# Keeping split weight pieces in DRAM between the two halves of the tokens

## The chip, the cores and the metric

The kernel runs on one core of a Trainium2 chip. The metric is the device time of one execution in microseconds. Engines are TensorE (PE, with its weight loads as PEld), VectorE (DVE), ScalarE (ACT), GpSimd (POOL) and SyncE (SP), which issues almost every DMA.

## The reference

One layer of a hybrid model with three branches on 2048 tokens of width 1024, in float32. Only the first lines matter for the change: the input projection to 8192 columns is the largest matrix product, and every branch reads pieces of it.

```python
h_lat = rmsnorm(x, norm_g) * (1.0 + sc_l) + sh_l
pl = split_proj(h_lat @ w_in + b_in)         # D_IN = 8192 columns
o_lat = neighbourhood_attention(q, k, v, k_c, v_c, rpb)   # 8 heads, 8 x 16 windows, 256 context keys
y_a = (a_b * short_conv(a_c * a_x, w_conv, b_conv) * silu(a_z)) @ w_br_a
y_f = (fourier_mix(f_u) * silu(f_z)) @ w_br_f
y_c = (attn_o * silu(c_z)) @ w_br_c
x_new = x + gt_l * ((sig(g_a) * y_a + sig(g_f) * y_f + sig(g_c) * y_c) @ w_out)
return rmsnorm(x_new, final_g)
```

## The kernel before

**Precision.** A float32 product is made of three matmuls of type fp32r. Each operand is split into a high part, which is a cast of it, and a low part, which is the operand less its high part. `split` (lines 130 to 132) does this: ScalarE casts (line 131), VectorE or GpSimd subtracts (line 132).

**The projection.** The 64 column blocks of w_in (128 columns each, 1024 deep, 512 KB) are taken two at a time. `pair(ma, mb, ...)` computes two blocks for 1024 tokens as a 2 by 2 block product with seven products in place of eight: the seven weight operands are a11, a12, a22 and four sums and differences of a11, a12, a21, a22, which GpSimd makes (lines 337 to 339 and 355). `piece` splits one of these into `wh` and `wl`, four buffers each; `P` runs its product, 12 matmuls over 512 tokens each (lines 310 to 312), into a PSUM bank; `evac` functions add the products together, apply bias and the nonlinearity, and store the result to DRAM. The token operands (B11, B21, B22, T1 to T4) are split once for each half of the tokens and stay in SBUF.

**The order of the work.** The tokens are done in two halves of 1024, and each half goes through the same 32 pairs: Q, K, V and the Fourier input, then the gated branches, then 12 gate pairs. In both halves every pair loads its two raw blocks from w_in (line 298, buffers `wr`, three of them) and makes and splits all seven pieces. Besides the pairs:

- start-up computes the modulation and normalises the first half, between the first two pairs (`first_pair`)
- in the first half, `small_work` makes gate vectors and the tables of the attention bias (`tbl`, line 736) between products
- near the end of the first half the token operands of the second half are made (`Prep`); the last pair of the half splits them in its hook
- in the second half, the 24 pairs after Q, K, V and Fourier run beside attention and then the Fourier transform, which are generators advanced by 2.7 steps for each product
- the last loop does the three branch products, the output product and the final norm for four blocks of 512 tokens

The framework places each engine's instructions in an order of its own, from a simulated time, and adds the waits; at run time each engine, and SP with its DMAs, goes through its list in order.

Of the kernel before, what the change touches and what calls it, by code (L numbers as in the profile page):

```python
# [11 lines left out]
F32 = mybir.dt.float32  # L12
F32R = mybir.dt.float32r
AF = mybir.ActivationFunctionType
ALU = mybir.AluOpType
# [44 lines left out]
def emit(tc, I, out, dbg=None):  # L60
    nc = tc.nc
# [4 lines left out]
    def pool(stack, name, bufs=1, space=None, side=None):  # L66
        kw = {} if space is None else {"space": space}
        if space is not DRAM:
            kw["reuse_waits"] = "tile"
        if side:  # L70
            return Aligned(stack, lambda n_, b_: tc.tile_pool(name=n_, bufs=b_, side=side, **kw), name, bufs)
        return stack.enter_context(tc.tile_pool(name=name, bufs=bufs, **kw))
# [4 lines left out]
    dr = pool(es, "dr", 1, DRAM)  # L77
# [4 lines left out]
    load = nc.sync.dma_start  # L82
    store = nc.sync.dma_start
    vtt = nc.vector.tensor_tensor
# [32 lines left out]
    state = {}  # L117
# [12 lines left out]
    def split(hi, lo, src, heng, leng):  # L130
        heng.copy(hi, src) if heng is nc.scalar else heng.tensor_copy(hi, src)  # L131
        return leng.tensor_tensor(lo, src, hi.bitcast(F32), ALU.subtract)  # L132
# [6 lines left out]
    wp = pool(ws_, "wp")  # L139
# [147 lines left out]

    def piece(src, leng, nm):  # L290
        wh = wp.tile([128, 512], F32R, tag="wh", name="wh" + nm, bufs=4)
        wl = wp.tile([128, 512], F32R, tag="wl", name="wl" + nm, bufs=4)
        split(wh, wl, src, nc.scalar, leng)
        return wh, wl

    def wraw_(m, p=None, bufs=3):
        t = (p or wp).tile([128, D], F32, tag="wr", name=f"wr{m}", bufs=bufs)
        load(t, I["w_in"][m])
        return t

    def wraw(m):
        t = wraw_(m)
        return t[:, :512], t[:, 512:]

    def prod(ps, w, name, first, last=True):
        op = state["op"]
        for k in KP:
            s = slice(k * 128, k * 128 + 128)
            oh, ol = op[name, k]
            nc.tensor.matmul(ps, w[0][:, s], oh, start=first and k == 0, stop=False)  # L310
            nc.tensor.matmul(ps, w[0][:, s], ol, start=False, stop=False)  # L311
            nc.tensor.matmul(ps, w[1][:, s], oh, start=False, stop=last and k == 3)  # L312

    def bank():
        return pm.tile([128, 512], F32, tag="mm", name="mm")

    def tmp():
        return wp.tile([128, 512], F32, tag="tp", name="tp", bufs=3)

    def P(w, name):  # L320
        p = bank()
        prod(p, w, name, True)
        return p

    def pair(ma, mb, evac, bg=None):
        bg = bg or (lambda: None)
        a11, a12 = wraw(ma)
        a21, a22 = wraw(mb)
        p = P(piece(a11, nc.vector, "1"), "B11")
        s1 = tmp()  # L330
        nc.scalar.copy(s1, p)
        bg()
        p = P(piece(a12, nc.vector, "2"), "B21")
        evac(0, 0, p, s1)
        bg()
        t1 = wp.tile([128, 512], F32, tag="ws", name="ws", bufs=1)
        ptt(t1, a21, a22, ALU.add)  # L337
        ptt(a21, a11, a21, ALU.subtract)
        ptt(a11, t1, a11, ALU.subtract)  # L339
        p = P(piece(a11, nc.vector, "6"), "T2")  # L340
        vtt(s1, p, s1, ALU.add)
        bg()
        p = P(piece(t1, nc.gpsimd, "5"), "T1")
        v = tmp()
        vtt(v, p, s1, ALU.add)  # L345
        bg()
        for _ in pair_end(evac, a11, a12, a21, a22, s1, v):
            bg()

    def pair_end(evac, a11, a12, a21, a22, u2, v):  # L350
        p = P(piece(a21, nc.gpsimd, "7"), "T3")
        evac(1, 1, p, v)
        vtt(u2, p, u2, ALU.add)  # L353
        yield
        ptt(a12, a12, a11, ALU.subtract)  # L355
        p = P(piece(a12, nc.gpsimd, "3"), "B22")
        evac(0, 1, p, v)
        yield
        p = P(piece(a22, nc.vector, "4"), "T4")
        evac(1, 0, p, u2)  # L360
        yield

    def first_pair(ma, mb, evac, raw, s1, t5):

        w = raw(ma)
        a11, a12 = w[:, :512], w[:, 512:]
        yield
        p = P(piece(a11, nc.vector, "1"), "B11")
        nc.scalar.copy(s1, p)
        yield  # L370
        w = raw(mb)
        a21, a22 = w[:, :512], w[:, 512:]
        yield
        t1 = wp.tile([128, 512], F32, tag="ws", name="ws", bufs=1)
        ptt(t1, a21, a22, ALU.add)
        ptt(a21, a11, a21, ALU.subtract)
        ptt(a11, t1, a11, ALU.subtract)
        p = P(piece(t1, nc.vector, "5"), "T1")
        vtt(t5, p, s1, ALU.add)
        yield  # L380
        p = P(piece(a12, nc.vector, "2"), "B21")
        evac(0, 0, p, s1)
        yield
        p = P(piece(a11, nc.vector, "6"), "T2")
        vtt(s1, p, s1, ALU.add)
        vtt(t5, p, t5, ALU.add)
        yield
        yield from pair_end(evac, a11, a12, a21, a22, s1, t5)


    def pre(dst, ps, add, m):
# [172 lines left out]
    def mod_end(k):  # L564
        row = rows.pop(k)
        pc_ = pe1.tile([128, 2, 2], F32, tag="pc", name="pc_")
        for s in range(2):
# [4 lines left out]
    state["op"], state["half"] = Operands(), 0  # L572
    raws = (lambda m: wraw_(m), lambda m: wraw_(m, ep, 2))
    gens = [first_pair(M_Q + 2 * n, M_Q + 2 * n + 1, ev_q((2 * n, 2 * n + 1)), raws[n],
                       tmp(), tmp() if n else scratch("T4", "l", 3, "t5"))
            for n in range(2)]
# [112 lines left out]
    for n_, p in enumerate(prs[2:]):  # L689
        (pair(*p))  # L690
        if n_ == 1:
            ex.close()
        if n_ >= 1:
            for m in (M_K, M_V):
                if n_ < 5:
                    ctx_tile(m + n_ - 1)
# [62 lines left out]
    for n_, p in enumerate(rest[:16]):  # L759
        (pair(*p, bg=lambda: bgs(0.5)))  # L760
# [31 lines left out]
    for p in rest[16:-1]:  # L792
        pair(*p, bg=lambda: bgn(RH))
# [390 lines left out]
    def load_wb(j, n_):  # L1184
        wr = c2.tile([128, 512], F32, tag="wr", name="wr", bufs=WRB)
        nc.sync.dma_start(wr, I["w_br"][j, n_])
        wh = c2.tile([128, 512], F32R, tag="wbh", name="wbh", bufs=3)
        wl = c2.tile([128, 512], F32R, tag="wbl", name="wbl", bufs=3)
        split(wh, wl, wr, nc.scalar, nc.gpsimd)
        return wh, wl  # L1190
# [31 lines left out]
    for b in range(NB):  # L1222
# [5 lines left out]
        for j in range(8):  # L1228
            acc = None
            for n_, br in enumerate("afc"):  # L1230
                wh, wl = wb0.pop(0) if wb0 else load_wb(j, n_)
# [134 lines left out]
```

## Time and profile before

| | |
|---|---|
| median of 3 runs | 2255.39 us (2252.5 to 2258.48) |
| profiled execution | 2256.13 us, span 2254.4 us |
| mean granted clock of TensorE | 0.985 |
| DMA | 336.78 MB, 149 GB/s on the mean |

The profile is taken from one execution. Busy time of an engine is the union of its instructions; a matmul of 512 columns is listed with about 0.39 us, but the next starts 0.23 us after it, so matmuls overlap in the list. A wait is put down to the instruction that released it. The granted clock is the share of full speed (2.4 GHz) that TensorE was given.

### The profile page before, as it was taken

What the parts mean: (1) busy time and instruction counts of PE and PEld (TensorE: products, weight loads), DVE (VectorE), ACT (ScalarE), POOL (GpSimd) and SP (SyncE); (2) the same over time, 40 slices, a digit from 0 to 9 for tenths busy, and PEclk for the clock granted to TensorE, in tenths of its full rate; (3) what the DMA queues carried; (4) which work ended last, traced back from release to release, by engine and by line L of the source; (5) the groups of instructions that cost most, each with busy time, mean ns of one, the idle gap of its engine ahead of it and who ended that gap; (6) DMA issues with size and microseconds to landing.
All of it is one profiled execution on the core that took longest, in us unless ns stands there. A gap on an engine that the chain in (4) does not pass through costs nothing. (4 is left out here: it accounts for less than half of the span.)

```text
span 2254.4 us, 32033 instructions
## 1 busy us (share of the span) xinstructions
PE 2132.9 (95%) x10588; PEld 1686.6 (75%) x10588; DVE 1547.0 (69%) x2731; ACT 887.1 (39%) x2011; POOL 1011.5 (45%) x761
## 2 busy tenths in 40 slices
PE   6899989999999899999999999999999898999998
PEld 4678768888788687777777777777757677878777
DVE  6864685565665665778787788786736868787773
ACT  3443222334544442454555555554213332222121
POOL 2753467654464654444444334343415243434341
PEclk8999999999999899999999999999999999999999
DMA  6244644233233344343444444453466676666561
GB/s 255 80 136 117 225 174 168 94 108 117 94 101 111 101 142 131 109 126 107 142 127 127 139 148 127 141 149 127 154 211 218 212 223 214 192 206 191 173 190 67
DMA packets 198863, 336.78 MB, mean 149 GB/s; under 512 B 22249, under 2 KB 89129, under 8 KB 197546
## 3 DMA queue, kind: packets, MB, share of 16 engines
q1 hardware_dynamic: 198554, 334.47, 46.8%
q8 instruction: 84, 1.38, 0.3%
q14 instruction: 81, 0.66, 0.1%
q10 hardware_dynamic: 144, 0.26, 0.0%
HBM read 248.27 MB, written 86.38 MB: 148 GB/s over the span
## 5 line engine op out<-in xcount | busy, mean ns | idle before, releaser
L131 ACT CAST wh<-wr 128x512 fp32r<-128x512 f32 x384 | 237.7, 620 | 479.1 <-PE mm L311 388.1
L132 DVE TENSOR_TENSOR wl<-wr,wh 128x512 fp32r<-128x512 f32 x256 | 244.7, 957 | 37.0 <-ACT wh L131 36.8
L132 POOL TENSOR_TENSOR wl<-wr,wh 128x512 fp32r<-128x512 f32 x128 | 173.7, 1360 | 212.8 <-ACT wh L131 191.0
L337 POOL TENSOR_TENSOR ws<-wr 128x512 f32<-128x512 f32 x62 | 89.0, 1435 | 309.0 <-DMA wr<-w_in 255.3
L395 DVE SCALAR_TENSOR_TENSOR st<-mm,bin,tp 128x512 f32<-128x512 f32 x158 | 118.0, 747 | 143.0 <-PE mm L312 136.0
L132 POOL TENSOR_TENSOR wbl<-wr,wbh 128x512 fp32r<-128x512 f32 x96 | 130.9, 1367 | 163.0 <-ACT wbh L131 160.4
L126 PE MATMUL mm<-yh,wbh 128*128 128x512 f32 x384 | 153.5, 400 | 17.8 <-DVE tg L1238 10.4
L128 PE MATMUL mm<-yh,wbl 128*128 128x512 f32 x384 | 152.8, 398 | 2.3 <-POOL wbl L132 2.3
L127 PE MATMUL mm<-yl,wbh 128*128 128x512 f32 x384 | 151.8, 396 | 0.3 <-DVE yl L132 0.3
L931 PE MATMUL tr<-ident,P 128*128 128x128 f32 (+3 forms) x672 | 120.4, 280 | 19.1 <-DVE PT L941 7.9
L132 POOL TENSOR_TENSOR wl<-ws,wh 128x512 fp32r<-128x512 f32 x62 | 83.7, 1350 | 112.5 <-ACT wh L131 94.8
L931 PEld LDWEIGHTS tr<-ident,P 128*128 128x128 f32 (+3 forms) x672 | 78.9, 139 | 68.4 <-DVE PT L941 25.4
L355 POOL TENSOR_TENSOR wr<-wr 128x512 f32<-128x512 f32 x64 | 87.9, 1373 | 93.7 <-DVE wl L132 58.8
L450 DVE TENSOR_TENSOR st<-mm,tp 128x512 f32<-128x512 f32 x96 | 65.9, 686 | 87.2 <-PE mm L312 84.4
L310 PE MATMUL mm<-B11h,wh 128*128 128x512 f32 x256 | 104.5, 408 | 14.0 <-DVE tp L353 7.4
L131 ACT CAST wbh<-wr 128x512 fp32r<-128x512 f32 x96 | 59.2, 620 | 127.6 <-PE mm L127 61.0
L126 PE MATMUL po<-wo,mh 128*128 128x512 f32 x256 | 101.2, 395 | 7.8 <-DVE xn L1261 7.7
L310 PE MATMUL mm<-T4h,wh 128*128 128x512 f32 x256 | 103.1, 403 | 4.5 <-DVE tp L345 4.5
L311 PE MATMUL mm<-B11l,wh 128*128 128x512 f32 x256 | 103.0, 402 | 4.2 <-DVE B11l L132 4.2
L339 POOL TENSOR_TENSOR wr<-ws,wr 128x512 f32<-128x512 f32 x62 | 84.3, 1360 | 49.6 <-DVE wl L132 36.3
L310 PE MATMUL mm<-B21h,wh 128*128 128x512 f32 x256 | 102.6, 401 | 3.6 <-DVE st L450 2.8
L310 PE MATMUL mm<-T2h,wh 128*128 128x512 f32 x256 | 102.8, 402 | 1.4 <-ACT T2h L131 1.4
(319 smaller groups left out, 6293.3 us busy)
## 6 DMA issues: line engine op xcount, KB each, us to landing
wr<-w_in SPq DMA_DIRECT2D x136, 512.0 KB
gd<-st SPq DMA_DIRECT2D x96, 256.0 KB
wr<-w_br SPq DMA_DIRECT2D x96, 256.0 KB
tg<-gd SPq DMA_DIRECT2D x96, 256.0 KB
tab<-dft SPq DMA_DIRECT2D x40, 256.0 KB
wa<-w_ada SPq DMA_DIRECT2D x32, 256.0 KB
rawq<-qd SPq DMA_DIRECT2D x64, 128.0 KB
rawk<-kd SPq DMA_DIRECT2D x64, 128.0 KB
```

Of the source, the lines that this page charges most:

```text
L126: nc.tensor.matmul(ps, ah, bh, start=first, stop=False)
L127: nc.tensor.matmul(ps, ah, bl, start=False, stop=False)
L128: nc.tensor.matmul(ps, al, bh, start=False, stop=last)
L131: heng.copy(hi, src) if heng is nc.scalar else heng.tensor_copy(hi, src)
L132: return leng.tensor_tensor(lo, src, hi.bitcast(F32), ALU.subtract)
L310: nc.tensor.matmul(ps, w[0][:, s], oh, start=first and k == 0, stop=False)
L311: nc.tensor.matmul(ps, w[0][:, s], ol, start=False, stop=False)
L337: ptt(t1, a21, a22, ALU.add)
L339: ptt(a11, t1, a11, ALU.subtract)
L355: ptt(a12, a12, a11, ALU.subtract)
L395: stt(dst, ps, bc(m), add, ALU.add, ALU.add)
L931: nc.tensor.transpose(pt[:w_, x * 128 : x * 128 + 128], src, ident)
```

## The change

In the first half `piece` splits into the two parts of one tile `w2` (four buffers) and stores that tile, 512 KB, into a DRAM tile of its own. In the second half `pair` makes no pieces: `pair_again` loads the kept piece for each of its seven products. Four of seven loads go to the buffers of `w2`, three to those of `wr`, which the raw blocks no longer need. The context keys and values (`ctx_tile`) still split their pieces, without a store. The products, their order and the evacuations are the same in the second half.

```diff
+    kept = {}
+
+    def piece(src, leng, nm, keep=None):
+
+        w = wp.tile([128, 2, 512], F32R, tag="w2", name="w2" + nm, bufs=4)
+        split(w[:, 0], w[:, 1], src, nc.scalar, leng)
+        if keep is not None:
+            kept[keep, nm] = d = dr.tile([128, 2, 512], F32, name=f"wd{keep}_{nm}")
+            store(d, w.bitcast(F32))
+        return w[:, 0], w[:, 1]
+
+    turn_ = iter(range(10 ** 6))
+
+    def again(ma, nm):
+        if next(turn_) % 7 < 4:
+            w = wp.tile([128, 2, 512], F32R, tag="w2", name="w2k", bufs=4)
+        else:
+            w = wp.tile([128, 2, 512], F32R, tag="wr", name="wrk", bufs=3)
+        load(w.bitcast(F32), kept[ma, nm])
+        return w[:, 0], w[:, 1]
...
     def pair(ma, mb, evac, bg=None):
         bg = bg or (lambda: None)
+        if state["half"]:
+            for _ in pair_again(ma, evac):
+                bg()
+            return
         a11, a12 = wraw(ma)
         a21, a22 = wraw(mb)
-        p = P(piece(a11, nc.vector, "1"), "B11")
+        p = P(piece(a11, nc.vector, "1", ma), "B11")
...
+    def pair_again(ma, evac):
+        p = P(again(ma, "1"), "B11")
+        s1 = tmp()
+        nc.scalar.copy(s1, p)
+        yield
+        p = P(again(ma, "2"), "B21")
+        evac(0, 0, p, s1)
+        yield
...
```

The other calls of `piece` in `pair`, `pair_end` and `first_pair` get the key `ma` in the same way, and `pair_again` goes on through the pieces 6, 5, 7, 3 and 4.

## Rows read from the trace of the kernel before

**Rows 1.** The page: span, then busy us, share of the span and instructions.

```profile
span 2254.4 us, 32033 instructions
...
PE 2132.9 (95%) x10588; PEld 1686.6 (75%) x10588; DVE 1547.0 (69%) x2731; ACT 887.1 (39%) x2011; POOL 1011.5 (45%) x761
```

**Rows 2.** Busy time by stage: stage, length, engines with instructions, granted clock, DMA share, GB/s.

```profile
0.00:115.00 115.00, 86.77 (x369) 68.82 (x369) 84.28 (x131) 49.45 (x85) 58.03 (x48) 0.93 0.48 168
...
240.00:353.00 113.00, 103.78 (x447) 81.39 (x447) 82.18 (x104) 29.10 (x51) 66.09 (x44) 0.98 0.62 213
353.00:582.00 229.00, 229.00 (x1012) 189.60 (x1012) 125.75 (x157) 82.45 (x133) 133.87 (x97) 1.00 0.33 110
582.00:758.00 176.00, 163.60 (x711) 133.65 (x710) 124.85 (x167) 87.73 (x145) 97.13 (x68) 0.95 0.30 98
758.00:918.00 160.00, 155.25 (x700) 127.59 (x699) 84.39 (x110) 56.65 (x103) 82.48 (x63) 1.00 0.43 132
918.00:1562.00 644.00, 622.42 (x3939) 476.28 (x3937) 515.08 (x1295) 346.15 (x1061) 266.90 (x204) 1.00 0.44 130
...
1704.00:1765.00 61.00, 59.62 (x269) 48.63 (x267) 44.30 (x74) 23.20 (x38) 28.41 (x21) 1.00 0.64 204
1765.00:1800.00 35.00, 26.77 (x101) 19.15 (x99) 27.48 (x41) 13.23 (x22) 8.38 (x6) 0.90 0.72 234
```

**Rows 3.** Waits of weight loads, 918 to 1562 us: total us, times, longest.

```profile
PEld po L953 <- issue: 35.1, 154, 0.4
PEld tr L931 <- DVE PT L941: 25.2, 65, 1.6
...
PEld tr L931 <- ACT PT L941: 6.4, 22, 0.5
PEld tr L931 <- DVE P L897: 6.3, 5, 2.8
```

**Rows 4.** Order of time in one gate pair of the first half.

```profile
563.68 1.30 POOL L132 TENSOR_TENSOR wl<-ws,wh 128x512 fp32r<-128x512 f32 x1 [1.75 <-ACT wh L131]
...
570.44 0.33 SPq L298 DMA_DIRECT2D wr<-w_in  x1
...
571.11 0.39 PE L310 MATMUL mm<-T1h,wh 128*128 128x512 f32 x1
...
573.83 0.39 PE L310 MATMUL mm<-T3h,wh 128*128 128x512 f32 x1
...
574.64 0.69 DVE L132 TENSOR_TENSOR wl<-wr,wh 128x512 fp32r<-128x512 f32 x1
574.64 1.82 POOL L337 TENSOR_TENSOR ws<-wr 128x512 f32<-128x512 f32 x1 [4.23 <-DMA wr<-w_in]
```

**Rows 5.** Groups of instructions, 758 to 1765 us: busy us, mean ns, idle before.

```profile
L131 ACT CAST wh<-wr 128x512 fp32r<-128x512 f32 x190 | 117.6, 620 | 215.5 <-PE mm L311 197.8 <-POOL wr L339 6.0 <-PE mm L312 4.3
L132 DVE TENSOR_TENSOR wl<-wr,wh 128x512 fp32r<-128x512 f32 x126 | 114.4, 908 | 13.7 <-ACT wh L131 13.6
...
L132 POOL TENSOR_TENSOR wl<-wr,wh 128x512 fp32r<-128x512 f32 x64 | 83.2, 1302 | 148.0 <-ACT wh L131 126.2 <-PE sl L886 5.6 <-DMA vt<-vd 5.3
L338 POOL TENSOR_TENSOR wr<-wr,wr 128x512 f32<-128x512 f32 x31 | 45.5, 1466 | 2.4
...
L132 POOL TENSOR_TENSOR wl<-ws,wh 128x512 fp32r<-128x512 f32 x32 | 41.9, 1308 | 86.9 <-ACT wh L131 69.9 <-PE sl L886 8.6 <-PE sx L883 4.8
L131 ACT CAST wh<-ws 128x512 fp32r<-128x512 f32 x32 | 19.8, 620 | 22.2 <-PE mm L311 22.2
```

**Rows 6.** The VectorE splits beside attention, 918 to 1562 us (four a pair).

```profile
L132 DVE TENSOR_TENSOR wl<-wr,wh 128x512 fp32r<-128x512 f32 x68 | 62.0, 912 | 0.0
```

**Rows 7.** Busy time in two shorter stretches, columns as in the stages above.

```profile
240.00:263.00 23.00, 23.00 (x114) 18.91 (x114) 13.32 (x17) 8.41 (x16) 14.36 (x11) 1.00 0.76 261
747.00:758.00 11.00, 7.21 (x16) 4.75 (x17) 9.28 (x12) 3.72 (x7) 6.33 (x5) 0.51 0.31 101
```

**Rows 8.** Waits of VectorE for the bias tables, 240 to 353 us.

```profile
DVE Bv L735 <- DMA tbl<-Bv: 9.7, 7, 2.3
```

More of the change, by code (lines that the diff above doesn't have):

```diff
@@ L332, in pair @@
         bg()
-        p = P(piece(a12, nc.vector, "2"), "B21")
+        p = P(piece(a12, nc.vector, "2", ma), "B21")
         evac(0, 0, p, s1)
@@ L339, in pair @@
         ptt(a11, t1, a11, ALU.subtract)
-        p = P(piece(a11, nc.vector, "6"), "T2")
+        p = P(piece(a11, nc.vector, "6", ma), "T2")
         vtt(s1, p, s1, ALU.add)
         bg()
-        p = P(piece(t1, nc.gpsimd, "5"), "T1")
+        p = P(piece(t1, nc.gpsimd, "5", ma), "T1")
         v = tmp()
@@ L346, in pair, with pair_end @@
         bg()
-        for _ in pair_end(evac, a11, a12, a21, a22, s1, v):
+        for _ in pair_end(ma, evac, a11, a12, a21, a22, s1, v):
             bg()
-    def pair_end(evac, a11, a12, a21, a22, u2, v):
-        p = P(piece(a21, nc.gpsimd, "7"), "T3")
+    def pair_end(ma, evac, a11, a12, a21, a22, u2, v):
+        p = P(piece(a21, nc.gpsimd, "7", ma), "T3")
         evac(1, 1, p, v)
@@ L355, in pair_end @@
         ptt(a12, a12, a11, ALU.subtract)
-        p = P(piece(a12, nc.gpsimd, "3"), "B22")
+        p = P(piece(a12, nc.gpsimd, "3", ma), "B22")
         evac(0, 1, p, v)
         yield
-        p = P(piece(a22, nc.vector, "4"), "T4")
+        p = P(piece(a22, nc.vector, "4", ma), "T4")
         evac(1, 0, p, u2)
+        yield
[6 more added lines that the diff above has]
+        evac(0, 0, p, s1)
+        yield
+        p = P(again(ma, "6"), "T2")
+        vtt(s1, p, s1, ALU.add)
+        yield
+        p = P(again(ma, "5"), "T1")
+        v = tmp()
+        vtt(v, p, s1, ALU.add)
+        yield
+        p = P(again(ma, "7"), "T3")
+        evac(1, 1, p, v)
+        vtt(s1, p, s1, ALU.add)
+        yield
+        p = P(again(ma, "3"), "B22")
+        evac(0, 1, p, v)
+        yield
+        p = P(again(ma, "4"), "T4")
+        evac(1, 0, p, s1)
         yield
@@ L367, in first_pair @@
         yield
-        p = P(piece(a11, nc.vector, "1"), "B11")
+        p = P(piece(a11, nc.vector, "1", ma), "B11")
         nc.scalar.copy(s1, p)
@@ L377, in first_pair @@
         ptt(a11, t1, a11, ALU.subtract)
-        p = P(piece(t1, nc.vector, "5"), "T1")
+        p = P(piece(t1, nc.vector, "5", ma), "T1")
         vtt(t5, p, s1, ALU.add)
         yield
-        p = P(piece(a12, nc.vector, "2"), "B21")
+        p = P(piece(a12, nc.vector, "2", ma), "B21")
         evac(0, 0, p, s1)
         yield
-        p = P(piece(a11, nc.vector, "6"), "T2")
+        p = P(piece(a11, nc.vector, "6", ma), "T2")
         vtt(s1, p, s1, ALU.add)
@@ L387, in first_pair @@
         yield
-        yield from pair_end(evac, a11, a12, a21, a22, s1, t5)
+        yield from pair_end(ma, evac, a11, a12, a21, a22, s1, t5)
     def pre(dst, ps, add, m):
```

5 lines of the change are left out of this document (removed).

## The prediction

> **What bounds the kernel now.** The page comes first. The profiled execution took 2256.13 us for a span of 2254.4 us [rows 1], 0.7 us above the median of the three runs, so the sum below is made on it and needs no correction. TensorE is busy for 95% of the span, VectorE for 69% [rows 1]. An average says little here, so the second view is busy time by stage [rows 2]. The reader is to see three kinds of stage in it. In the gate pairs of the first half (353 to 582 us) TensorE is busy for all of 229 us at full clock: nothing that another engine gives up can shorten this. In the second half the Q, K, V and Fourier pairs (758 to 918) and the pairs that run beside attention (918 to 1562) leave 4.8 and 21.6 us of TensorE idle. And there are three places where pairs hand over to other work: start-up (0 to 115), the change of operands (582 to 758, 12.4 us idle) and the entry into the last loop (1765 to 1800, 8.2 us idle). The third view is the stall list of the attention stage [rows 3]; the fourth is the order of time of one gate pair [rows 4], to see how much time a piece has between its split and its product.
>
> A pair is seven products, each of 12 matmuls. In the gate stage a product starts every 573.83 - 571.11 = 2.72 us [rows 4], so a pair costs 19.04 us and cannot go below that; 64 pairs are 1219 us of the span. The change touches none of it. What it can win is idle time of TensorE in the second half; what it can lose is that full stage in the first.
>
> **What is removed.** In the second half all 32 pairs lose seven splits and four differences each. Between 758 and 1765 us that is 117.6 us of ScalarE casts with 19.8 us more on the fourth piece, 114.4 us on VectorE, 83.2 and 41.9 us of splits and four groups of differences, the largest of 45.5 us, on GpSimd [rows 5]. This is work of engines that do not set the end, so by itself it is worth nothing: TensorE covers it. It counts only where TensorE waits for these queues. The 64 loads of w_in in that half, 0.52 MB each, go too.
>
> **Attention stage.** The view of stalls names, for the idle time of weight loads, 25.2 us for a VectorE copy of transposed probabilities, 6.4 for the same copy on ScalarE and 6.3 for the probabilities, 37.9 us together; 35.1 us more stand at the small value products with no releaser, and nothing here changes those [rows 3]. TensorE itself was idle for 644 - 622.4 = 21.6 us [rows 2]; a weight load hides behind the matmul before it, so the true loss lies between 21.6 and 37.9 us, say 30. Why are those copies late? VectorE is busy for 515 of 644 us, and 68 splits of 912 ns, 62.0 us, stand in the same queue [rows 2, 6]; GpSimd's splits and differences end too. With an eighth of VectorE's work gone I take half of the 30: **-15 us**. The bounds are 0 (the copy is a round trip of transposes, copy, transposes that no empty queue shortens) and -38.
>
> **Handovers.** At the change of operands VectorE is the chain: it is busy for 9.3 of the 11 us from 747 to 758, and TensorE runs at a granted clock of 0.51, its lower level of 1.2 GHz, right after it had stood still [rows 7]. In that queue, between the splits of the new operands, stand the first splits of the first Q pair, which the change turns into loads. Four of them at 0.69 us, the row at 574.64 of the gate pair being the unhindered split [rows 4], are 2.8 us: **-3 us**, bounds 0 and -6. At the entry into the last loop the hook of the last pair shares VectorE, ScalarE and GpSimd with seven splits; of 8.2 us idle [rows 2] I take **-3 us**, bounds 0 and -8. The stages 758 to 918 and 1704 to 1765 have under 5 and 2 us idle [rows 2]; I cost them at nothing.
>
> **What is added in the first half: 224 stores of 0.52 MB.** A pair then stores 7 x 0.524 = 3.67 MB. How fast can the queue go? From 240 to 263 us it moves 261 GB/s at a busy share of 0.76, from 353 to 582 us 110 GB/s at 0.33 [rows 2, 7]; both make 330 to 343 GB/s when full. In the gate stage the stores add 3.67 MB in 19.04 us, 193 GB/s: 303 GB/s, a share near 0.9. It fits, with little room. Two things have to hold. The raw weights must still come in time: a load issued at 570.44 let GpSimd start at 574.64, 4.2 us later [rows 4], for a piece whose product is still two products away in the next pair. And a slot of the split pieces is now free only when its store has landed as well. The split that begins on GpSimd at 563.68 ends 1.30 us later; its product runs from 571.11 to 573.83 [rows 4]. So the store has 8.8 us, where a load of the same size took 4.2 in a queue with a store in it. While that holds, TensorE covers the store: gate stage **0**, bounds 0 and +8.
>
> From 240 to 353 us it does not fit. There the queue already moves 213 GB/s [rows 2], for the bias tables and the modulation weights among others, and five pairs (its 447 matmuls hold five times 84) add 5 x 3.67 MB in 113 us, 162 GB/s: 375 against 343, nine parts in a hundred too much, +10.5 us if the stage stretched with it. VectorE waits there for tables to land, 9.7 us in seven waits [rows 8], so it would feel it. But the stage is not bound by the queue at every moment, and what is late can drain after 353: **+5 us**, bounds 0 and +33 (below). The Trainium skill speaks against the change here. Its page "DMA: Bandwidth & Descriptors", section Bandwidth, holds that for transfers between HBM and SBUF the memory side binds, at some 358 GB/s for a core; by that the stage would stretch by 375/358, an estimate of +5.4 us, and the sum would be 2243.5 us. No row here shows more than 261 GB/s over a pair, so the trace neither confirms nor refutes that figure.
>
> Start-up (0 to 115 us, share 0.48, TensorE idle for 28 us [rows 2]) gets the first stores between loads of weights and x on the one SP queue. A store that waits for its split holds what is issued behind it. **+2 us**, bounds 0 and +8.
>
> **What is added in the second half.** Seven loads a pair in place of two: 2.62 MB more. Beside attention 17 pairs take 644 us [rows 6], so 69 GB/s on 130, a share of 0.44 x 199/130 = 0.67. The loads have seven slots, so each is issued nearly a pair ahead, 16 us or more; they are covered. Attention's own small loads queue behind them: **+1 us**, bounds 0 and +6. From 1704 to 1765 204 GB/s become 342, full [rows 2], but the last pair's loads are out one pair, 19 us, before the stage ends. In the Fourier stage (1562 to 1704) a slower load of 1 MB and a freer VectorE cancel: 0. Each load waits on SP for the product seven back, and the loads and stores behind it wait too; TensorE would feel that first in attention, and it is in the +6.
>
> **Sum.** 2256.13 - 15 - 3 - 3 + 0 + 5 + 2 + 1 = 2243.1 us, 0.6% less. A difference of 0.3% (6.8 us) is about what a measurement of this kernel can tell from none.
>
> **The rivals.**
> *Slower, by the store slots.* If a store lands later than the 8.8 us that it has, the slot is late, the next split is late, and TensorE stops. Four slots turn in 4 x 2.72 = 10.9 us; with a landing of 12 us a turn takes 3.2 us more, 29%. In a queue that is asked for 375 GB/s a landing of 12 us is thinkable between 240 and 353: 113 x 0.29 = +33 us, in place of my +5: 2271 us. From a landing of about 10.4 us on (+16 us) it outweighs the gains. Against it: stores issue one in 2.7 us, and elsewhere the queue has room.
> *No difference.* The copies of transposed probabilities wait for their own transposes, VectorE is as late as before, and the gains are the handovers alone: 2256.13 - 6 + 8 = 2258 us. For it: 35.1 us of the idle time have no releaser at all. Against it: a split of 912 ns is longer than most waits that it can cause.
> *A larger gain.* All 37.9 us of named waits go and the handovers give their bounds of 6 and 8 us, with +8 lost: 2256.13 - 51.9 + 8 = 2212 us. Against it: VectorE keeps seven eighths of its work. Weight loads fill 189.6 of 229 us in the gate stage, 83%, and 476 of 644 beside attention, 74% [rows 2]; if attention came up to 83%, 69 us would go: 2187 us. The matmuls of attention are shorter, so I give that 0.03 of this rival's chance. The Trainium skill's page "Perfetto Trace Analysis", section Identifying the Most-Contended Engine, has that share and not the busy time of matmuls as the measure of headroom, and so speaks for this case.
>
> **How the numbers follow.** Forecast (2230 to 2249 us) 0.42, larger gain 0.15, no difference 0.19, slower 0.24. So faster by over 0.3% 0.57, within 0.3% 0.19, slower 0.24. The range has to reach into both signs: from 2214, near the larger gain, to 2268, near the slower rival. The forecast's own range is 2230 to 2249.
>
> **What would show it.** Right: 353 to 582 still holds 19.04 us a pair; the pairs beside attention come closer than 37.9 us, and the waits of weight loads for VectorE's copies fall from 25.2 us to half; GpSimd is nearly idle in the second half but for keys. Wrong: splits on ScalarE in the first half that wait for a store to w's kept copy; GpSimd waiting for w_in far longer than 4.2 us; TensorE under 100% in the gate stage, or at its lower clock after such waits; in the second half, TensorE waiting for a piece's load.

## The result and the profile after

The changed kernel takes 2349.71 us (median of 4 runs, 2346.68 to 2355.19) against 2253.94 for the kernel before on the same chip: a ratio of 1.0428, interval 1.0397 to 1.0458. It is 4.3% slower where 0.6% faster was forecast, and lies far outside the range.

The head of the page of the changed kernel answers to [rows 1]; its line of the SyncE queue (queue, packets, MB, share of 16 engines) is added.

```profile
span 2350.1 us, 31854 instructions
...
PE 2181.7 (93%) x10588; PEld 1717.3 (73%) x10588; DVE 1404.5 (60%) x2603; ACT 753.2 (32%) x1787; POOL 696.0 (30%) x537
...
q1 hardware_dynamic: 253850, 535.82, 68.1%
```

The work went as the diff says: VectorE loses 143 us, ScalarE 134, GpSimd 316. TensorE has the same 10588 matmuls. All of the gain is in engines that do not set the end, and 95.7 us of span came on top. Only 46.9 us of them are idle time of TensorE (121.5 us before, 168.4 after). The other 48.8 us are its busy time: the same matmuls took longer, at a mean granted clock of 0.967 where it was 0.985, so a stop costs more than its own length.

Where they came from is seen when each pair's first product is laid beside the same one of before. The table gives the lag (start of the pair after, less start before), from the starts of the matmuls of the product B11 in the two traces. Pairs are counted from 0; 0 to 31 are the first half.

| pair | start before | lag | what lies between it and the row above |
|---|---|---|---|
| 7 | 240.2 | +8.2 | start-up, Q, K, V |
| 12 | 353.5 | +12.6 | tables of before (274 to 338 us) |
| 21 | 524.9 | +44.3 | nine pairs of 19.0 us before, 20.5 to 24.3 after |
| 23 | 563.0 | +44.3 | two gate pairs of 19.0 us |
| 26 | 628.7 | +55.7 | loads of x for the second half |
| 31 | 724.0 | +55.7 | five pairs |
| 33 | 775.8 | +51.0 | change of operands |
| 40 | 918.2 | +46.3 | rest of Q, K, V, Fourier input |
| 44 | 1070.3 | +41.8 | first four pairs of attention |
| 57 | 1562.0 | +91.4 | thirteen pairs beside attention |
| 60 | 1675.2 | +78.3 | Fourier transform |
| 63 | 1745.0 | +86.2 | last pairs |
| end | 2254.4 | +95.7 | last loop |

So there are two main losses: some 44 us in the first half before the pair at 525 us, with 11 more at the loads of x, and 50 us beside attention. The Fourier transform gives 13 us back, and from pair 60 to the end 17 us are lost again. (The stretch from 353 to 582 us, which the prediction calls the gate stage, holds eight pairs of the other branches and the first four gate pairs.)

Busy time by stage in the changed kernel, columns as in [rows 2]:

```profile
344.00:569.00 225.00, 205.53 (x840) 163.80 (x841) 130.66 (x155) 60.74 (x106) 114.99 (x83) 0.95 0.75 282
569.00:607.00 38.00, 38.00 (x169) 31.50 (x168) 15.66 (x22) 15.14 (x25) 15.85 (x14) 1.00 0.87 321
684.00:780.00 96.00, 96.00 (x426) 79.55 (x427) 51.78 (x73) 39.85 (x65) 53.78 (x40) 1.00 0.81 303
...
964.00:1653.00 689.00, 646.24 (x3938) 491.10 (x3937) 446.48 (x1227) 281.32 (x941) 100.17 (x85) 0.98 0.63 187
```

The reader is to see what does not fit a simple bound by bandwidth. TensorE is full at 569 to 607 us with 321 GB/s, share 0.87, and idle for 19.5 of 225 us at 344 to 569 with only 282 GB/s, share 0.75. Attention moves 187 GB/s, share 0.63, and loses 45 us over this window. The granted clock fell where TensorE stood still in between, to 0.95 and 0.98 on the mean from 1.00. Waits in the stretch 344 to 569 (engine, line, released by: total us, times, longest):

```profile
POOL ws L356 <- DMA wr<-w_in: 103.7, 11, 11.6
...
ACT w L131 <- POOL wr L358: 54.0, 10, 7.7
ACT w L131 <- DMA wr<-w_in: 40.7, 8, 14.0
...
ACT w L131 <- DMA wd<-w: 11.1, 7, 2.4
```

The same first wait in 353 to 582 us of the kernel before:

```profile
POOL ws L337 <- DMA wr<-w_in: 41.2, 10, 4.6
```

The prediction's rival, splits that wait for the store of their slot, is the last line of after: 11.1 us. What grew is the wait for raw weights, from 4.1 to 9.4 us each time. The casts wait for the same blocks and differences. TensorE itself waits for VectorE, which evacuates the products late (its own largest wait, 42.7 us, is for the casts), and its weight loads wait for the casts:

```profile
PE mm L325 <- DVE st L440: 15.3, 7, 2.9
...
PEld mm L325 <- ACT w L131: 13.6, 6, 5.4
```

The order of time shows why it does not catch up:

```profile
448.80 1.08 SPq L298 DMA_DIRECT2D wd<-w  x1
449.93 1.88 SPq L313 DMA_DIRECT2D wr<-w_in  x2
451.91 1.03 SPq L781 DMA_DIRECT2D tbl<-Bv  x2
...
458.22 1.29 POOL L356 TENSOR_TENSOR ws<-wr 128x512 f32<-128x512 f32 x1 [10.81 <-DMA wr<-w_in]
...
469.24 2.55 POOL L132 TENSOR_TENSOR w<-wr,w 128x512 fp32r<-128x512 f32 x2
...
474.21 1.20 SPq L313 DMA_DIRECT2D wr<-w_in  x1
...
481.98 1.29 POOL L356 TENSOR_TENSOR ws<-wr 128x512 f32<-128x512 f32 x1 [10.20 <-DMA wr<-w_in]
```

Two raw blocks are issued from 449.93 on (the row holds both; the second starts at 450.66) and let GpSimd start at 458.22, some 8 us later, where before it was 4.2 [rows 4]. GpSimd makes the differences and its last splits, to 471.79. Only then is the buffer of the older block free; the next load goes out at 474.21, with the stores of the pieces just made issued before it, and its data let GpSimd start at 481.98. One turn takes 481.98 - 458.22 = 23.8 us in place of 19.04. The queue's own view over 448 to 484 us, in 40 slices of 0.9 us (busy tenths, then GB/s), shows the other side of the turn:

```profile
DMA  9999988989999930000009999999899997999999
GB/s 391 433 399 425 328 205 223 300 237 332 407 428 417 396 137 5 0 0 9 0 0 387 410 428 389 421 428 423 332 428 397 409 259 218 310 396 408 414 426 395
```

and three windows of it, columns as above:

```profile
461.00:466.00 5.00, 2.10 (x10) 1.47 (x9) 2.84 (x3) 1.14 (x2) 4.84 (x4) 0.98 0.03 13
448.00:461.00 13.00, 12.87 (x56) 10.00 (x55) 8.42 (x12) 1.77 (x3) 2.71 (x2) 1.00 0.96 346
466.00:482.00 16.00, 16.00 (x64) 13.10 (x65) 10.43 (x14) 5.91 (x10) 5.17 (x6) 0.90 0.94 358
```

The queue is full, then empty for five us in which GpSimd works and TensorE stands still for most of the time, then full again. GpSimd waits while the burst passes, and the queue waits while GpSimd works: nothing in this loop runs ahead. A mean share of 0.75 hides a queue that is full for most of each turn.

In the other half the waits of VectorE, 964 to 1653 us, have two lines that were small before:

```profile
DVE P L936 <- DMA bt<-tbl: 24.0, 12, 3.7
...
DVE T L903 <- DMA rawq<-qd: 16.3, 15, 2.5
```

Before, in 918 to 1562 us, there is no wait for `bt` and the other is this:

```profile
DVE T L858 <- DMA rawq<-qd: 2.4, 1, 2.4
```

So both halves show the same kind of wait: small or urgent loads that land late on the queue that carries the pieces. The traces show the waits; the experiments have to show what causes them.

### The profile page after: what moved, and what is told of

It reads as the page before. It is cut to its first block, busy times and chain, and to the rows that moved or that the text cites. A ratio compares the mean times of both kernels' runs of the same rounds, so it can differ in the third digit from the quotient of the medians.

```text
span 2350.1 us, 31854 instructions
## 1 busy us (share of the span) xinstructions
PE 2181.7 (93%) x10588; PEld 1717.3 (73%) x10588; DVE 1404.5 (60%) x2603; ACT 753.2 (32%) x1787; POOL 696.0 (30%) x537
## 5 line engine op out<-in xcount | busy, mean ns | idle before, releaser
L132 POOL TENSOR_TENSOR KL<-rawk,KH 128x384 fp32r<-128x384 f32 (+1 forms) x64 | 76.8, 1209 | 494.1 <-ACT KH L131 407.4
L131 ACT CAST w<-wr 128x512 fp32r<-128x512 f32 x192 | 116.7, 620 | 304.5 <-POOL wr L358 125.5
L132 DVE TENSOR_TENSOR w<-wr,w 128x512 fp32r<-128x512 f32 x128 | 115.1, 905 | 118.7 <-ACT w L131 114.0
L496 ACT ACTIVATE st<-st,binh 128x512 f32<-128x512 f32 x96 | 69.4, 722 | 157.3 <-DVE st L495 151.0
L126 PE MATMUL po<-wo,mh 128*128 128x512 f32 x256 | 101.5, 397 | 14.2 <-DVE xn L1306 12.2
L936 DVE CUSTOM_DVE_ANT_0 P<-sl,bt,sm 128x480 f32<-128x480 f32 (+5 forms) x128 | 76.8, 600 | 41.4 <-DMA bt<-tbl 24.0
L128 PE MATMUL po<-wo,ml 128*128 128x512 f32 x256 | 100.6, 394 | 0.4 <-DVE ml L132 0.4
L132 POOL TENSOR_TENSOR w<-wr,w 128x512 fp32r<-128x512 f32 x64 | 88.3, 1393 | 41.3 <-ACT w L131 40.0
L127 PE MATMUL po<-wo,mh 128*128 128x512 f32 x256 | 100.2, 391 | 0.0
L986 DVE COPY PT<-tr 128x384 f32<-128x384 f32 x128 | 70.7, 552 | 40.5 <-PE tr L976 38.2
L126 PEld LDWEIGHTS mm<-yh,wbh 128*128 128x128 f32 x384 | 73.5, 192 | 28.7 <-issue 11.3
```

What stands on the lines that cost most here:

```text
L126: nc.tensor.matmul(ps, ah, bh, start=first, stop=False)
L127: nc.tensor.matmul(ps, ah, bl, start=False, stop=False)
L128: nc.tensor.matmul(ps, al, bh, start=False, stop=last)
L496: nc.scalar.activation(t, t, AF.Tanh, bias=bch(M_G + j), scale=0.5)
L936: nc.vector.tensor_tensor_reduce(Pl, sl[:, :n], bt[:, :n], 1.0, sm[:, 0:1], ALU.add, ALU.max, accum_out=sm[:, 1:2])
L986: eng.copy(d_, s_) if eng is nc.scalar else eng.tensor_copy(d_, s_)
```

## Experiments

Diffs are against the changed kernel. Ratios are to the kernel before, with 95% intervals.

**The parts alone.** One tile for both parts without stores or loads; stores alone; loads alone.

```diff
 e1:  in pair():  -  if state["half"]: ... pair_again ... return
      in piece(): -  if keep is not None:   +  if False:
 e2:  in pair(): as e1
      in piece(): +  if keep is not None and not state["half"]:
 e3:  in piece(): +  if keep == M_Q:
      in again(): -  load(w.bitcast(F32), kept[ma, nm])
                  +  load(w.bitcast(F32), kept[M_Q, nm])
```

> Control: both parts of a piece are in one tile, nothing is stored or loaded, both halves split as before. If the loss of 4.3% came from the joint tile (a slot is free only when the whole product has ended) or from the order of instructions that goes with it, this is slower by 1% or more. If the transfers do it, it is within 0.3% of the kernel before, some 2254 us.

> The 224 stores in the first half alone; the second half makes its pieces as before, and no kept piece is read. Theory 1 (stores put other transfers of the first half late, above all the raw weights): the first half loses what it lost in the changed kernel, 45 to 60 us, and the second half loses nothing: 2300 to 2315 us. Theory 2 (the loss belongs to the second half, and the first only shifts): under 2275 us.

> The loads in the second half alone: only the seven pieces of the first pair are stored, and every pair of the second half loads these same seven, so its products are of the wrong weights while sizes and count of the loads are those of the change. Theory 1 (loads put attention's own small loads late): the first half is that of before, and the attention stage grows by 35 to 50 us, with 5 to 15 us won at the handovers: 2280 to 2300 us. Theory 2 (attention was slow only because the stores had shifted the work): 2235 to 2250 us, a gain.

e1: 2254.03 us, 0.9993 [0.9978, 1.0009]: the tile is free. e2: 2307.7 us, 1.0245 [1.0223, 1.0268], +54 us, all of it in the first half, with the shape of the table above. e3: 2293.63 us, 1.0180 [1.0158, 1.0201], +40 us: 13 us ahead of before at pair 44, then 33 us behind at pair 57. The two add to 95 of the 95.7 us, so on SyncE's queue the two losses add up.

**How much is stored.** 224 stores of 8 KB; then of 256 KB (the high part).

```diff
 as e2, and in piece():
-            store(d, w.bitcast(F32))
 e4: +            store(d, w.bitcast(F32)[:, 1:2, 496:512])
 e9: +            store(d, w.bitcast(F32)[:, 0:1])
```

> Like the stores alone, but each of the 224 stores takes 16 columns of the low part, 8 KB in place of 512 KB, so the list of SyncE has the same entries and waits with next to no bytes. If it is the entries and their waits for the splits that hold back what stands behind them, the loss is that of the full stores, 2300 us or more. If it is the bytes in the queue, the time is within 0.5% of the kernel before, under 2265 us.

> The 224 stores alone on SyncE, but of the high part only, 256 KB each, half the bytes. If every stored byte costs the same wherever it falls, half of the 54 us is lost, some 27 us: 2277 to 2285 us. If the loss comes from the queue being nearly full (269 to 297 GB/s between 250 and 700 us with the full stores), well under half is lost: up to 2268 us. If it is a cost of each store whatever its size, 2300 us or more, which the run with small stores already speaks against.

e4: 2251.22 us, 0.9997 [0.9982, 1.0013]. e9: 2256.49 us, 1.0009 [0.9998, 1.0020]. The order written for TensorE is nearly the same in e2, e4 and e9. So neither the 224 issues nor the waits of stores for their splits cost anything; nor does half the amount. The second half of the bytes costs 52 us. The sums that write the bias tables (count: shortest, median, longest ns, first and last start) show the step; before, e9, e2:

```profile
L735 DVE TENSOR_TENSOR Bv<-R,rm x24: 691/886/1983, 274.4 to 337.1; 128x528 f32<-128x528 f32 x16, 128x704 f32<-128x704 f32 x8
```

```profile
L776 DVE TENSOR_TENSOR Bv<-R,rm x24: 694/1084/1973, 303.9 to 368.8; 128x528 f32<-128x528 f32 x16, 128x704 f32<-128x704 f32 x8
```

```profile
L776 DVE TENSOR_TENSOR Bv<-R,rm x24: 707/964/1972, 340.0 to 495.5; 128x528 f32<-128x528 f32 x16, 128x704 f32<-128x704 f32 x8
```

At 256 KB the tables come 30 us later and take as long as before (65 us for 63). At 512 KB they take 155 us, through most of the pairs that lose. That spread is not a matter of the queue alone: it stands in the order that the framework wrote. Counted in VectorE's subtractions of pieces, four a pair, these sums stand between the 37th and the 49th before, the 41st and the 53rd in e9, and the 46th and the 74th in e2 and in the change: over three pairs, three and seven. So e9 and e2 differ in the bytes and in this order, and the next runs have to say which of them counts.

**Another queue, in the first half.** Stores issued by ScalarE; loads of w_in issued by GpSimd; stores of the tables issued by GpSimd.

```diff
 as e2, and
 e5:  -  store(d, w.bitcast(F32))              +  nc.scalar.dma_start(d, w.bitcast(F32))
 e6:  -  load(t, I["w_in"][m])                 +  nc.gpsimd.dma_start(t, I["w_in"][m])
 e16: -  store(tbl[v, :, x, : ND * w], bv)     +  nc.gpsimd.dma_start(tbl[v, :, x, : ND * w], bv)
```

> The 224 stores alone, as before, but issued by ScalarE, so they stand in another DMA queue than the raw weights, on the same 16 engines. Theory 1a (the raw weights are late because they stand behind stores in SyncE's own queue): the loss of 54 us falls to less than half, under 2280 us. Theory 1b (what counts is the bytes that the 16 engines move, whoever issued them): the loss stays, 2300 to 2315 us. ScalarE must now wait in its own list for the subtractions of VectorE and GpSimd, which can cost by itself: above 2320 us would be that.

> The 224 stores alone on SyncE, and the raw weights of both halves loaded by GpSimd, which does most of the splits that free their buffers. Theory 1a: raw weights land as they did without stores, and the loss falls to less than half, under 2280 us. Theory 1b: 2300 us or more. If the bias tables, not the raw weights, are what is late, the loss stays too, and GpSimd's waits for w_in are short while VectorE's waits for tables remain.

> As the run with the 224 stores alone (2307.7 us, +54), but the 24 stores of the bias tables are issued by GpSimd. If the tables' place behind the pieces in SyncE's queue is what draws the loss out to 500 us, they end before 430 us and the loss falls to +15 to +35: 2270 to 2290 us. If it is the raw weights alone that are late behind the stores, the loss stays at +45 to +60: 2299 to 2314 us.

e5: 2295.43 us, 1.0167 [1.0151, 1.0184]. e6: 2302.88 us, 1.0204 [1.0187, 1.0222]. e16: 2298.29 us, 1.0192 [1.0175, 1.0209]. By the ratios each gives back 9 to 18 us, none more. e5 falls between its two theories. By the lag at pair 33, after the change of operands, the first half loses 41.5, 34.5 and 47.2 us in them where e2 loses 57.5; e6 loses 13 more in the second half, whose raw blocks GpSimd issues too.

e6 tests the reading of the traces above. From 344 to 569 us GpSimd waits for raw blocks no longer than before, but VectorE waits longer for the tables than the 9.7 us of [rows 8]:

```profile
POOL ws L352 <- DMA wr<-w_in: 40.7, 10, 6.1
```

```profile
DVE Bv L776 <- DMA tbl<-Bv: 25.9, 11, 4.7
```

This is the third case of its expectation: 23 us of the first half come back with the raw blocks, and the larger part of the loss stays. (GpSimd also waits 15.3 us for VectorE's splits before it issues these loads, which may hide some.)

e5 and e16 speak against the order of the tables. In e5 they stand at their place of before (37th to 49th subtraction, 288 to 363 us), and the first half loses 41.5 us even so. In e16 they stand from the 46th to the 57th and end at 411 us, as its first theory asked, but the loss stays near the second (+46, where e9 with the tables over as few pairs and half the bytes has +2); 15 us of it come between pair 14 (422 us) and pair 21, after the last table. GpSimd, which now issues the stores of the tables in its own order, waits 24.2 us for the sums between 330 and 420 us, and the pairs there take up to 29.9 us.

In e5 some 17 of the 41 us fall between pair 7 and pair 14, where the DMA engines are nearly full. Its busy time by stage:

```profile
250.00:300.00 50.00, 44.47 (x189) 35.52 (x188) 31.68 (x40) 12.01 (x22) 23.20 (x17) 0.90 0.91 336
300.00:400.00 100.00, 85.23 (x357) 66.55 (x355) 61.95 (x78) 22.54 (x40) 52.53 (x39) 0.98 0.87 332
```

From its pair 17 on (lag 27.8) the pairs run at 19.04 us up to the loads of x. So the place behind the stores in SyncE's queue is not the whole cause here: where tables, modulation weights, raw blocks and pieces come together the DMA engines themselves are near full, and what is moved to another queue makes a new wait. How the 57 us divide beyond this stays open.

**Fewer pairs kept.** The twelve gate pairs; then the last 20 pairs, from the 13th on, with the loads issued by ScalarE, and by GpSimd.

```diff
 in pair():   +  if (ma, "1") in kept and state["half"]:
 in piece():
 e12:       +  if keep is not None and keep >= M_G and not state["half"]:
 e13, e15:  +  if keep is not None and state.get("keep") and not state["half"]:
            (set to n_ >= 4 in the loop over rest[:16])
 in again():
 e12, e13:  +  nc.scalar.dma_start(w.bitcast(F32), kept[ma, nm])
 e15:       +  nc.gpsimd.dma_start(w.bitcast(F32), kept[ma, nm])
```

> Only the 12 gate pairs keep their pieces (stores on SyncE, from some 353 us on, after the tables), and their 84 loads in the second half are issued by ScalarE; the other 20 pairs split twice as before. If the loss of the stores belongs to the stretch with the tables, the stores cost 10 us at most and the gates' share of the second half, some 15 to 20 us of the 35 after the handover, gives it back or more: 2238 to 2256 us. If each store costs the same, 84 of 224 lose 20 us: 2255 to 2268 us.

> Only the last 20 pairs of the half are kept, from the 13th on (353 us before, when the bias tables have been stored at 275 to 339 us); the 12 pairs before them are made in both halves; the loads are issued by ScalarE. If the loss of the first half needs the tables, the modulation weights and the pieces together in SyncE's queue, the 12 pairs from 353 us on run at 19.0 us again, and attention and the last loop gain what the loads on ScalarE's queue gave (about -10 each): 2234 us, between 2230 and 2244. If each pair that stores its seven pieces costs 2 to 4 us of itself, as pairs 13 to 22 did in the change, the first half loses 25 to 40: about 2265 us.

> As the run with the last 20 pairs kept, but the loads of the second half are issued by GpSimd. If ScalarE's own work holds its loads or is held by their waits for buffers, this is 3 to 12 us less; if any queue apart from SyncE's does the same, within 3 us of it.

e12: 2250.69 us, 0.9984 [0.9968, 1.0000]. e13: 2258.52 us, 1.0024 [1.0007, 1.0041]. e15: 2267.13 us, 1.0055 [1.0037, 1.0073]. What counts is the first half, where all these stores are on SyncE. In e12 the lag never leaves -1.1 to +0.1 us up to pair 31. In e13 and e15 it goes from -2.1 and +0.5 at pair 12 to +6.3 and +8.4 at pair 31, and most pairs hold 19.0 us. e13 from 344 us on:

```profile
344.00:505.00 161.00, 156.63 (x682) 128.48 (x681) 89.29 (x110) 49.97 (x87) 91.17 (x66) 0.99 0.77 292
505.00:569.00 64.00, 63.45 (x280) 52.28 (x279) 31.39 (x41) 23.87 (x40) 32.28 (x25) 1.00 0.85 315
```

It moves more than the changed kernel did there (292 and 315 GB/s against 282) and loses 8 us up to pair 31 where that lost 43 from pair 12. So full stores are nearly free where the tables are done and the loop enters without a lag; e13 changes both at once. The loss of e16 after its last table speaks for the lag. The expected gain in the second half did not come: e13 stays 3 to 8 us behind through attention, and pairs 60 to 62 cost 8 us more. In e12 the pairs with loads lose 10 us (lag -3.8 at pair 52, +6.8 at pair 62) before the last loop gives 9 back. e15, expected within 3 us of e13 or below it, is 9 us above.

**Another queue, and other amounts, in the second half.** Loads issued by ScalarE; loads of 256 KB on SyncE; the seven pieces loaded once and held.

```diff
 as e3, and in again():
 e7:  -  load(w.bitcast(F32), kept[M_Q, nm])
      +  nc.scalar.dma_start(w.bitcast(F32), kept[M_Q, nm])
 e14: -  load(w.bitcast(F32), kept[M_Q, nm])
      +  load(w[:, 0:1].bitcast(F32), kept[M_Q, nm][:, 0:1])
      +  return w[:, 0], w[:, 0]
 e8:  +  if nm in held:
      +      return held[nm]
      ...
      +  held[nm] = w[:, 0], w[:, 1]
```

> The loads of kept pieces alone (always those of the first pair, so wrong weights), issued by ScalarE in place of SyncE. Theory 1a (attention's bias and query loads are late because they stand behind loads of 512 KB in the one queue): the attention stage falls back to that of before or below, 2235 to 2265 us. Theory 1b (bytes on the engines): 2285 us or more.

> As the run with the loads alone on SyncE (2293.6 us, +40), but every load of the second half takes only the high part of a piece, 256 KB, which is then used for both parts of the weight (so the product is not the reference's). Instructions, their waits and their order on SyncE stay. If it is the bytes in SyncE's queue that make attention's own loads late, most of the loss goes: 2220 to 2245 us. If it is the waits of the loads for their buffers, which hold what SyncE issues behind them, the loss stays: 2280 to 2295 us.

> Second half with neither splits nor loads: the seven pieces of the first pair are loaded once, one into each slot, and used by all 32 pairs (wrong weights). It shows what the second half can gain at most. By the prediction's terms (15 beside attention, 6 at the handovers) 2225 to 2240 us. If splits cost attention nothing, only the handovers are won: 2240 to 2250 us. If a new order of instructions is what slows attention, it is slow here too: 2270 us or more.

e7: 2240.81 us, 0.9936 [0.9914, 0.9958], -16. e14: 2223.52 us, 0.9864 [0.9847, 0.9881], -29. e8: 2216.44 us, 0.9817 [0.9802, 0.9831], -40. So, each against the kernel before on its own chip, the same loads cost 81 us more than none on SyncE's queue (+40.4 and -40.3), 24 on ScalarE's, and at half the bytes 11 on SyncE's. e14 issues as many loads as e3 and each waits for the same buffer, so these waits on SyncE are not enough to make the loss; it comes with the bytes.

One reserve: [The change] calls the order of the products in the second half the same, and in the program's text it is, but the framework counts bytes and queues when it writes the order of each engine. For TensorE beside attention e8 and e14 are close, and the kernel before and e7 differ from them a little. e3 and the changed kernel have one and the same order, which is further from all of these (from pair 44 to pair 57 as many matmuls of attention in all, but 172 of them beside pair 47 in place of 151). No run has that order without the 512 KB loads on SyncE, or these loads with the other order. How much of the 81 us the order makes stays open.

One stretch of attention, 1070 to 1550 us, in e3, e7, e14 and e8:

```profile
1070.00:1550.00 480.00, 441.77 (x2686) 333.43 (x2685) 304.23 (x839) 196.52 (x649) 66.02 (x56) 0.98 0.62 186
```

```profile
1070.00:1550.00 480.00, 469.37 (x3001) 361.66 (x3001) 343.60 (x933) 219.35 (x724) 74.12 (x62) 1.00 0.69 206
```

```profile
1070.00:1550.00 480.00, 470.22 (x2978) 362.46 (x2977) 334.98 (x908) 215.70 (x708) 69.80 (x59) 0.99 0.53 157
```

```profile
1070.00:1550.00 480.00, 472.22 (x3014) 365.80 (x3013) 345.95 (x917) 215.96 (x709) 72.88 (x62) 1.00 0.37 112
```

TensorE gets through 2686 matmuls with 186 GB/s on one queue and 3001 with 206 GB/s on two. VectorE's waits name the late transfers, bias tiles and queries: 42.0 us in e3, where the lag grows by 46 us beside attention, and 10.2 in e7. e3 in 918 to 1595 us, e7 in 918 to 1551:

```profile
DVE P L936 <- DMA bt<-tbl: 25.2, 13, 3.9
DVE T L903 <- DMA rawq<-qd: 16.8, 16, 2.2
```

```profile
DVE T L903 <- DMA rawq<-qd: 5.8, 4, 2.2
...
DVE P L936 <- DMA bt<-tbl: 4.4, 5, 1.5
```

**The whole change on other queues.** Loads by ScalarE; loads and stores by ScalarE.

```diff
 e10, e11: -  load(w.bitcast(F32), kept[ma, nm])   +  nc.scalar.dma_start(w.bitcast(F32), kept[ma, nm])
 e11:      -  store(d, w.bitcast(F32))             +  nc.scalar.dma_start(d, w.bitcast(F32))
```

> The change itself, with right weights, but the kept pieces are loaded by ScalarE; the stores stay on SyncE. If the two halves add up, the stores' loss of 54 us and the gain of 16 us of the loads on that queue give 2290 to 2297 us, some 55 us less than the changed kernel. If stores and loads hurt each other, more than 2305 us.

> The change with stores and loads both issued by ScalarE. By adding up, 39 - 16 us over the kernel before: 2274 to 2282 us. Still slower than before, because the bytes of the stores saturate the queue while the bias tables are built.

e10: 2300.16 us, 1.0205 [1.0190, 1.0220]. e11: 2293.69 us, 1.0170 [1.0155, 1.0185]. Half of the loss goes with the loads; the first half keeps 48.1 and 43.2 us of lag at pair 33. Both miss what was expected by adding up, e10 by 3 us and e11 by 12: on other queues the two parts do not simply add.

**Low parts alone.** VectorE's four subtractions a pair become four loads of 256 KB; casts, differences and GpSimd's splits stay. Loads by SyncE, and by ScalarE.

```diff
 pair() as in e2; in piece(), for the pieces 1, 2, 6 and 4:
+        if low and state["half"]:
+            nc.scalar.copy(w[:, 0], src)
 e17: +            load(w[:, 1:2].bitcast(F32), kept[keep, nm])
 e18: +            nc.scalar.dma_start(w[:, 1:2].bitcast(F32), kept[keep, nm])
+            return w[:, 0], w[:, 1]
...
+            store(d, w.bitcast(F32)[:, 1:2])
```

> A version that stays inside the amounts that cost nothing (256 KB stores in the first half, under 2.1 MB of loads a pair in the second): only the low part of the four pieces that VectorE splits (1, 2, 6, 4) is stored, 4 x 256 KB a pair. In the second half raw blocks, differences, ScalarE's casts and GpSimd's splits stay; VectorE's four subtractions a pair become four loads of 256 KB on SyncE. If VectorE's queue was what attention waited for, and the amounts decide what the transfers cost, the first half loses 0 to 8 and the second gains 10 to 25: 2233 to 2248 us. If the casts and GpSimd's work that went with the held pieces were what counted, or the loads' waits for their buffers hold SyncE, no gain: 2252 to 2265 us.

> As the run with the low parts kept, but these loads are issued by ScalarE. If SyncE has room for 2.1 MB a pair, as the 256 KB loads say, this is within 5 us of it or up to 10 us more (ScalarE still casts, and waits in order); if the loads crowd SyncE, it is 5 to 20 us less.

e17: 2270.23 us, 1.0063 [1.0046, 1.0080]. e18: 2255.43 us, 1.0008 [0.9987, 1.0028]. The first half is free (lag +0.5 and -1.7 us through pairs 13 to 24), as the amounts said. The second half misses the expectation: e17 is 8.0 us ahead at pair 44 and 8.8 behind at pair 57. Its stretch of attention:

```profile
1070.00:1550.00 480.00, 455.32 (x2849) 346.72 (x2849) 345.84 (x892) 253.74 (x773) 185.95 (x145) 0.99 0.54 157
```

That is e14's rate to the GB/s, with 15 us more of TensorE idle. So the rate on the queue does not settle it alone; in e17 ScalarE and GpSimd still make pieces, and more urgent raw blocks stand in the same queue. e18 answers a part: with the same loads issued by ScalarE the lag beside attention (pairs 40 to 57) goes from +0.5 to -1.4 us, where in e17 it goes from -5.5 to +8.8, and the time is 15 us less, as expected for loads that crowd SyncE. (The orders written for these two differ as well, less than those of e3 and e7.) Why e18 is no faster than before stays open.

## Why the prediction was wrong

**The stores, the failed step of the first half.** The step was "gate stage 0, bounds 0 and +8", with +5 before it and "what is late can drain after 353". Between 240 and 353 us the lag grew from 8.2 to 12.6 us, +4.4 for +5, but by luck: the queue did not carry there what the term had put there. Only 3 of the 24 stores of tables were issued between 240 and 366 us of the changed kernel, and the tables, at 274 to 338 us before, were made at 341 to 497, by the new order that the framework wrote. Start-up gave +3.1 at pair 2 (113 us) for +2; the stretch from there to 240 us, which has no term, gave 5 more. Then the stretch costed at nothing lost 39 us (lag 12.6 at pair 12, 52.1 at pair 24).

I had checked the mean load, 303 GB/s against 330 to 343, and the slots of the stores. Both held: the rate is carried elsewhere at full TensorE (321 GB/s), and the slots cost 11 us of waits on ScalarE. What I named as the first condition, that raw weights come in time, I took as met by a landing of 4.2 us in a queue that was a third full. It became 8, in a loop of load, difference, split and release in which GpSimd and the queue take turns. e6 gives this condition's share, 23 of 57 us; the rest comes with the bytes (e9) and is not divided further. The tables had moved into the stage as well. e12 and e13 show that the stage as I had pictured it, without the tables, does carry the stores.

The Trainium skill's page "DMA: Bandwidth & Descriptors", section Bandwidth, puts the limit at some 358 GB/s, and the sum by it was as wrong as mine. The same section of the Trainium skill gives the figure for both cores of a pair at work, and 425 GB/s as measured on one alone. The traces here, of one core, agree with the latter: the slices above reach 433 GB/s, the most over 50 us is 362 (e6, 430 to 480 us), and the kernel before already moves 416 GB/s over 20 us of start-up:

```profile
11.00:31.00 20.00, 16.19 (x83) 12.73 (x81) 10.81 (x27) 7.40 (x13) 1.03 (x1) 1.00 1.03 416
```

So 330 to 343 GB/s was not the full queue either, and where the prediction says that the trace neither confirms nor refutes 358, this row of it refutes it. By 416 the 375 GB/s asked between 240 and 353 would have fitted.

**The loads, the failed step of the second half.** The step was "each is issued nearly a pair ahead, 16 us or more; they are covered. Attention's own small loads queue behind them", at +1, bounds 0 and +6. The first sentence held, with TensorE's weight loads waiting 5.6 us for `w2k` in the whole of attention. The second named the mechanism and mis-sized it: beside attention (pairs 40 to 57) the changed kernel loses 45 us, and e3 against e8 is 81 us for the second half. VectorE's waits for bias tiles and queries, 42.0 us in e3, show the mechanism; the order that the framework wrote for these loads may hold a part. A share of 0.67 as a mean said nothing of how long a 128 KB load stands behind the 512 KB ones. The loads of the last pairs, costed at nothing, are a further part: from pair 60 to the end the changed kernel loses 17 us and e3 11.

The same page of the Trainium skill, section Issuing engines are not separate DMA queues, holds that starting transfers from several engines saves only the time to start them. By that e7 would be e3 less a little. The runs differ: 2240.8 against 2293.6 us for the same bytes on the same 16 engines, 2300.2 against 2349.7 in e10 and the change, 2255.4 against 2270.2 in e18 and e17. The measurements go against the rule each time; but the order written for the engines differs within each pair too, least in e17 and e18, so that the queue alone makes these differences is not shown.

**The gains.** -15, -3 and -3 were asked of free pieces, -21 in all; with the pieces held (e8) it is -40. Attention gains 18 us (pairs 40 to 57), the change of operands 4, the last loop 6, so these terms had the right size or half of it. The other pairs, costed at nothing, give 11. The change itself shows only the -6 at the operands. The larger gain, 2212 us, comes near e8's 2216.4 by luck: it asked 37.9 us of attention, which gave 18. The cause I gave, VectorE's queue, is not borne out: without VectorE's subtractions alone (e17, e18) there was no gain, though these runs carry loads in their place.

**The rivals.** Slower was the right sign by the wrong mechanism: store slots were given 33 us, and the slots were hardly waited for. (By the sum's own terms these slots would have outweighed the gains from +18 us on, not +16.) No rival had the raw weights, though the list of signs did: GpSimd waiting for w_in far longer than 4.2 us and TensorE under 100% in the gate stage both came.

## What to carry to other kernels

Before adding a transfer, list what else is on its queue and which of it someone waits for; the mean share says whether the bytes fit, not whether the urgent ones arrive. Where a buffer ring feeds a serial loop, take the landing time in the loaded queue and not in the one of before, and ask which other work will then slide into the stage. Where a framework writes the order of the engines from a simulated time, a change of transfers writes a new order: compare the two before putting a loss down to a queue. To trade engine work for bytes, test the amounts first (here 256 KB in place of 512 KB cost nothing in the first half and 11 us in the second). No version built here that computes the whole reference beats the kernel before by more than the 0.3% that can be told apart.

## What the hardware showed that was not expected

- The cost of the stores is no line through zero: 1.8 MB a pair cost nothing (1.0009), 3.7 MB 54 us, and the same 3.7 MB in the gate pairs alone nothing (lag -0.3 us at pair 31 of e12).
- With equal bytes the queue by which a load is issued was worth 56 us (e3, e7, each against its own before; their written order differs too) and 15 us (e17, e18, whose order differs less).
- The queue reaches 433 GB/s in 0.9 us, 416 over 20 us and 362 over 50 us, where the prediction took 330 to 343 as full.
- About half of the time lost is not idle: TensorE was busy for 48.8 us more with the same matmuls, at a mean granted clock of 0.967 against 0.985.
- Between 240 and 600 us 23 single issues on SyncE took over 0.9 us in the changed kernel and none before (0.33 in [rows 4]). What lengthens them is not shown.
